# A gated DeltaNet layer on one core: token norms behind the first projection, query norms between the inversion stages, substitution rows begun behind a pair's own fifth projection

## The chip, the cores and the metric

The kernel runs on one core of one Trainium2 chip. The metric is the time of one execution of the whole program on the device, in microseconds (us); lower is better. The core has five engines that work side by side and are held together by semaphores: PE (TensorE, matrix products, with PEld for its weight loads), DVE (VectorE), ACT (ScalarE), POOL (GpSimd) and SP, whose queue issues most DMA transfers here. Each engine takes its instructions strictly in the order in which they stand in its own queue: an instruction that waits holds up all that stand behind it on that engine.

## What is computed

One layer of a decoder on 2048 tokens of width 1024, in float32: a gated DeltaNet mixer and a squared-ReLU MLP, each behind an RMS norm, and a last RMS norm. Cut to what matters here:

```python
def gated_deltanet(h, w_in, conv_w, a_log, dt_bias, norm_w, w_out):
    proj = h @ w_in                                   # 1024 -> q, k, v, z (1024 each), b, a (8 each)
    qkv = silu(causal_depthwise_conv(proj[..., :3 * 1024], conv_w))   # 4 taps
    q, k = l2_normalize(q), l2_normalize(k)           # 8 heads of 128
    beta = sigmoid(b); g = -exp(a_log) * softplus(a + dt_bias)
    o = chunk_gated_delta_rule(q, k, v, beta, g)
    o = rms(o) * norm_w * silu(z)
    return o @ w_out

# inside a chunk: (lower + eye) x = rhs is solved, lower = strict(k_beta k^T * decay)
# from chunk to chunk: v_new = u - w S ; o = q_dec S + attn v_new ; S = S * g_last + k_dec^T v_new

x = x + gated_deltanet(rms_norm(x, norm_mix), ...)
x = x + square(relu(rms_norm(x, norm_mlp) @ w_up)) @ w_down
return rms_norm(x, norm_final)
```

## The kernel before

**Blocks.** The 2048 tokens are done in two blocks (`blk` 0 and 1) of 1024. A block runs the mixer, then the output projection and the MLP. The mixer (L585) goes over two half-blocks of 512 tokens (`s` = 0 and 1), and in each over four pairs of heads (`h` = 0, 2, 4, 6). So a block has eight pairs, numbered 0 to 7 here: 0 to 3 in the first half-block, 4 to 7 in the second. Chunks have 128 tokens, so a pair has eight chunks (two heads of four), and `NC` is 8.

**One pair.** Six projections come first, in the order k, q, v, two heads each. A projection is 24 PE products of 128x512 (L117 to L119: high and low halves of the split operands, three for each of eight slices of the width) into a `pj` bank in PSUM. Its result goes through the causal convolution: ACT copies it (L303) and scales it (L304), DVE adds three taps (L307), ACT takes a tanh (L310) and DVE multiplies (L311). After the third and the fourth projection the pair's key matrices are built (`key_matrices`: PE L429, DVE L431 to L439, into `mt`), and after the fourth the substitution is set up: `invert_diagonal` solves the 32x32 diagonal blocks row by row. ACT copies `mt` four times (L322, `xc`), DVE transposes (L325, `pr`), and then DVE runs 62 short instructions, a product L333 and a sum L335 for each of 31 rows, called **rows** below. The generator hands them out in 24 steps.

**The pair before.** While a pair's projections run, the pair before it is finished, piece by piece. A generator, `prepare2`, gives one piece after each projection: the inversion's stages (`invert`, L340: DVE L345, ACT L347 `tcm`, PE L365, ACT L367 `z`, PE L373 to L376, L386 and L392), then the transposes of keys and values (PE L469, ACT L472 `vt` and `kt`) and `qe` (L463 on POOL), then PE L478 with DVE L480. After the sixth projection comes `wind_up`: the earlier pair's two gate projections (PE into `pj`, ACT L536, DVE L537), its query norms (`query_norms`: ACT L450 squares q into `sq`, PE L452 sums with a column of ones, DVE L454 adds) and then its `chain`.

**The chain** is the recurrence over four chunks for both heads: PE L496 (k times state), DVE L498 (`y`), PE L505, ACT L507 (`vr`), PE L511, DVE L512 (the new state `S`), with PE L502 and L515 into the output, then ACT L521 and L530. Each step waits for the step before it on another engine. The new pair's rows are handed out between these steps (`fill`). The chain that is run while pair n+1 is current is called chain n: chains 0 to 6 of a block stand in the loop, and chain 7 behind it, with no rows.

**Token norms.** In the first half-block, each pair also prepares 128 tokens of the next half-block: the tokens `xt` are loaded, ACT squares them (L180), DVE forms 1/sqrt by L145 and the seven instructions of `rsqrt` (L130 to L139) and scales (L181, `xn`), and PE transposes (L186) into the two `po` banks, in two groups of four; ACT L189 and DVE L190 take the results.

**What sets the order.** The code is written in one sequence. A scheduler then gives each engine its queue: it goes by the place in that sequence and by its own idea of when operands are ready. So a call that is moved in the Python code moves instructions in all queues, and not only its own.

## Time and profile before

| | before |
|---|---|
| time, median of 3 runs | 2926.35 us (2920.66 to 2933.81) |
| time of the profiled execution | 2926.04 us |
| span of its instructions | 2924.3 us |
| mean granted TensorE clock | 0.978 of full speed |
| DVE busy | 1548.9 us, 53% |
| ACT busy | 1034.0 us, 35% |
| POOL busy | 731.9 us, 25% |

The busy times are those of one profiled execution, the rest of the table is from the runs. The views that follow with the next parts are of that execution. A row of a timeline gives the start in us from the span's start, the busy time, the engine, the line of the kernel, the operation, out<-in by the program's names, partitions x elements of each, and how many instructions it joins; in brackets stands how long the engine was idle ahead of it and what it waited for.

### The profile page before, as it was taken

The numbers are of one execution on the slowest core, as the hardware profiler recorded it, in microseconds if no ns is written. First come the engines' busy times: TensorE is split into PE (matmuls) and PEld (weight loads), VectorE is DVE, ScalarE is ACT, GpSimd is POOL, SyncE is SP. The second block draws the span as 40 slices with busy tenths as digits, with TensorE's granted clock in tenths as the row PEclk, the third lists the DMA queues.
The fourth block names the chain that finished last, engine by engine and source line by source line (L and its number), as shares of the span: only waits on it lengthen the run. The fifth ranks groups of instructions, "written<-read, shape, count | busy, mean of one in ns | idle before, by whom it ended". The sixth has DMA issues, their size and how long they took to land.

```text
span 2924.3 us, 40261 instructions
## 1 busy us (share of the span) xinstructions
PE 2768.4 (95%) x15352; PEld 2325.2 (80%) x15352; DVE 1548.9 (53%) x3846; ACT 1034.0 (35%) x2338; POOL 731.9 (25%) x646
## 2 busy tenths in 40 slices
PE   7688989999999999999998999999999999999998
PEld 6577777779888888888886778787888888888887
DVE  7777777763433233333487676766544333332335
ACT  3455555554221211211246655555423112112112
POOL 6334232110042332332211111111004323323321
PEclk9889999999999999999999999999999999999999
DMA  6544455456421111111253434434662111111111
GB/s 227 182 159 168 165 177 176 169 202 226 161 72 43 58 50 38 58 51 37 65 194 142 142 122 145 145 137 148 199 230 87 44 44 58 44 44 58 48 40 65
DMA packets 81842, 337.62 MB, mean 115 GB/s; under 512 B 8817, under 2 KB 17265, under 8 KB 60145
## 3 DMA queue, kind: packets, MB, share of 16 engines
q1 hardware_dynamic: 60528, 292.98, 29.9%
q10 hardware_dynamic: 21120, 42.08, 4.2%
q8 instruction: 120, 1.97, 0.3%
q14 instruction: 74, 0.60, 0.1%
HBM read 271.98 MB, written 63.05 MB: 115 GB/s over the span
## 4 chain that ended last, share of the span: by engine, by line
PE 65%; DVE 10%; ACT 7%; issue 2%; DMA 2%; ACTq 0%; POOL 0%; POOLq 0%; DVEq 0%
PE pj L117 11%; PE pj L118 11%; PE pj L119 11%; PE kq L118 8%; PE kq L119 8%; PE kq L117 8%; ACT xc L322 2%; DVE tmp L333 2%; DVE c L307 1%; DVE tt L335 1%; DMA orw<-o_d 1%; PE kq L505 1%; PE kq L511 1%; PE kq L496 1%; PE kq L429 1%
## 5 line engine op out<-in xcount | busy, mean ns | idle before, releaser
L117 PE MATMUL pj<-hh,w 128*128 128x512 f32 x2048 | 820.7, 401 | 0.7 <-ACT c L304 0.7
L118 PE MATMUL pj<-hh,w 128*128 128x512 f32 x2048 | 817.6, 399 | 0.0
L119 PE MATMUL pj<-hl,w 128*128 128x512 f32 x2048 | 812.5, 397 | 0.0
L119 PEld LDWEIGHTS pj<-hl,w 128*128 128x128 f32 x2048 | 389.6, 190 | 79.0 <-issue 0.6
L117 PEld LDWEIGHTS pj<-hh,w 128*128 128x128 f32 x2048 | 390.1, 190 | 78.2 <-ACT c L304 1.1
L118 PEld LDWEIGHTS pj<-hh,w 128*128 128x128 f32 x2048 | 391.5, 191 | 75.8 <-issue 0.4
L742 ACT ACTIVATE r<-pj 128x512 f32<-128x512 f32 x128 | 76.9, 601 | 1059.7 <-PE pj L119 1059.7
L119 PE MATMUL kq<-dl,uh 128*128 128x512 f32 x992 | 386.8, 390 | 0.0
L118 PE MATMUL kq<-dh,ul 128*128 128x512 f32 x992 | 386.7, 390 | 0.0
L117 PE MATMUL kq<-dh,uh 128*128 128x512 f32 x992 | 386.6, 390 | 0.0
L745 DVE TENSOR_TENSOR ul<-r,uh 128x512 fp32r<-128x512 f32 x128 | 128.7, 1006 | 480.4 <-ACT uh L744 480.4
L785 DVE TENSOR_TENSOR x<-kq,x 128x512 f32<-128x512 f32 x256 | 176.8, 691 | 225.8 <-PE kq L119 223.1
L307 DVE SCALAR_TENSOR_TENSOR c<-raw,cst,c 128x512 f32<-128x512 f32 x288 | 239.9, 836 | 76.9 <-ACT c L304 73.9
L90 POOL TENSOR_SCALAR w<-wr 128x1024 fp32r<-128x1024 f32 x106 | 114.9, 1084 | 602.8 <-PE pj L119 380.5
L91 POOL TENSOR_TENSOR w<-wr,w 128x1024 fp32r<-128x1024 f32 x106 | 263.8, 2489 | 7.1
L785 DVE TENSOR_TENSOR x1h<-kq,x1h 128x512 f32<-128x512 f32 x256 | 176.7, 691 | 155.7 <-PE kq L119 155.4
L90 POOL TENSOR_SCALAR dh<-wr 128x1024 fp32r<-128x1024 f32 x62 | 64.5, 1058 | 642.0 <-PE kq L118 614.3
L117 PEld LDWEIGHTS kq<-dh,uh 128*128 128x128 f32 x992 | 186.2, 188 | 40.4 <-DVE rm L145 1.4
L118 PEld LDWEIGHTS kq<-dh,ul 128*128 128x128 f32 x992 | 186.2, 188 | 39.4
L119 PEld LDWEIGHTS kq<-dl,uh 128*128 128x128 f32 x992 | 186.2, 188 | 38.8
L333 DVE TENSOR_TENSOR tmp<-tt,pr 128x2 f32<-128x2 f32 (+30 forms) x496 | 162.1, 327 | 9.9 <-POOL pr L326 0.5
L117 PE MATMUL pj<-w,hh 128*128 128x256 f32 x512 | 147.2, 287 | 8.2 <-DMA w<-wo 5.9
(305 smaller groups left out, 3840.5 us busy)
## 6 DMA issues: line engine op xcount, KB each, us to landing
w<-wi SPq DMA_DIRECT2D x96, 1024.0 KB, 4.9
wi<-w SPq DMA_DIRECT2D x32, 1024.0 KB, 4.8
wr<-in_w_up SPq DMA_DIRECT2D x64, 512.0 KB, 3.6
w<-wo SPq DMA_DIRECT2D x32, 1024.0 KB, 5.7
wr<-in_w_down SPq DMA_DIRECT2D x64, 512.0 KB, 3.6
wr<-in_w_in SPq DMA_DIRECT2D x32, 512.0 KB, 5.8
qe<-eg_d ACTq DMA_DIRECT2D x16, 512.0 KB, 3.8
o_d<-z2s ACTq DMA_DIRECT2D x32, 256.0 KB, 3.3
```

The lines of the kernel that those rows point to most:

```text
L90: pool.tensor_scalar(dst_h, src, 1.0, 0.0, op0=MULT, op1=ADD)
L91: pool.tensor_tensor(dst_l, src, dst_h.bitcast(F32), op=SUB)
L117: pe.matmul(ps, ah, bh, start=first and i == 0, stop=False)
L118: pe.matmul(ps, al, bh, start=False, stop=False)
L119: pe.matmul(ps, ah, bl, start=False, stop=last and i == n - 1)
L307: dve.scalar_tensor_tensor(dst, raw[:, k:k + HB], cw[:, 4 * f + k:4 * f + k + 1], dst, op0=MULT, op1=ADD)
L322: act.copy(xc[r], mt[r, :, 32 * b:32 * b + 32].rearrange("p t i -> p i t").unsqueeze(2) .to_broadcast([32, 32, R, NC]))
L333: dve.tensor_tensor(tmp[:, 0:n, 0:i + 1], tt[:, 0:n, 0:i + 1], pr[:, i, 0:i + 1].unsqueeze(1).to_broadcast([P, n, i + 1]), op=MULT)
L335: dve.tensor_reduce(tt[:, 0:n, i], tmp[:, 0:n, 0:i + 1], axis=mybir.AxisListType.X, op=ADD)
L742: act.activation(r, ps, AF.Relu)
L745: dve.tensor_tensor(ul[:, hs], r, uh[:, hs].bitcast(F32), op=SUB)
L785: dve.tensor_tensor(dst, ps, dst, op=ADD)
```

## The change

There are four edits. All line numbers in the text are those of the kernel before.

1. **Token norms.** The load of `xt` is issued at the head of a pair of the first half-block, ahead of its first weights, where it was issued after the first projection. The norm itself now begins after projection 1 (before: 2), and a `yield` after `xn` parts it from the transposes, which come with steps 3 and 4 (before: 2 and 4). In the second block 1/sqrt is one power on POOL (L148) in place of `rsqrt` on DVE.
2. **Query norms** move from `wind_up`, where they stood ahead of the chain, into `prepare2`, behind the second and the third stage of the inversion. The inversion's stages begin one projection later than before.
3. **Rows.** One step of the pair's own rows is handed out after its fifth projection, and six after the sixth. The single step ahead of the gate projections goes, and the chain's first `fill` has two steps in place of three.
4. **Pair 0's rows**, which had been run out at the end of pair 0, are handed out in pair 1, 12 steps after its first projection and 24 after its second.

```diff
-    def norm_transpose(i, src, xn, wcol, hh, hl, tag):
+    def norm_transpose(i, src, xn, wcol, hh, hl, tag, use_pool=False):
...
-        dve.tensor_scalar_mul(xn, src, rstd_of(ssq))
+        dve.tensor_scalar_mul(xn, src, rstd_of(ssq, use_pool))
+        yield
...
-        yield from invert(ap, u["mt"], u["tt"], ub, t64)
-        yield
+        for i, _ in enumerate(invert(ap, u["mt"], u["tt"], ub, t64)):
+            yield
+            if i in (1, 2):
+                query_norms(ap, u, q2, i - 1)
...
-            fill(3)
+            fill(2)
...
-                fill(1)
                 z = [gate(ap, hT, h, sb)]
                 for _ in stages:
                     pass
                 z.append(gate(ap, hT, h + 1, sb))
-                for j in range(HP):
-                    query_norms(ap, u, qkv[0], j)
...
-                    next(stages, None)
+                    if s == 0:
+                        xt = wp.tile([P, D], F32, name="xt", tag="xt", bufs=4)
+                        r0 = (sb + 1) * HB + h // HP * P
+                        sp.dma_start(xt, x[r0:r0 + P, :])
...
-                            next(stages, None)
+
+                            if s == 0 and h == HP and n < 3:
+                                for _ in range(12 * n):
+                                    next(rows_of, None)
+                            if not (s == 0 and h == HP and n == 1):
+                                next(stages, None)
...
                             if s == 0 and n == 1:
-                                xt = wp.tile([P, D], F32, name="xt", tag="xt", bufs=4)
-                                r0 = (sb + 1) * HB + h // HP * P
-                                sp.dma_start(xt, x[r0:r0 + P, :])
-                            if s == 0 and n == 2:
                                 xt_steps = norm_transpose(
-                                    h // HP, xt, wp.tile([P, D], F32, name="xn", tag="xt", bufs=4), nmix, *hT2, "po")
-                            if s == 0 and n in (2, 4):
+                                    h // HP, xt, wp.tile([P, D], F32, name="xn", tag="xt", bufs=4), nmix, *hT2, "po",
+                                    blk > 0)
+                            if s == 0 and n in (1, 3, 4):
                                 next(xt_steps)
+                            if n >= 5:
+                                for _ in range((1, 6)[n - 5]):
+                                    next(rows_of)
...
-                    for _ in rows_of:
-                        pass
+                    if prev is not None:
+                        for _ in rows_of:
+                            pass
```

What this does to the queues is shown at three places. The first is PE at the beginning of chain 4 of the first block, which finishes the first pair of the second half-block. Before, with `w_4443` the second gate projection and `w_4710` the next pair's first projection:

```order
L119 MATMUL pj<-hl,w_4443 128x512
L452 MATMUL kq<-ones,sq 128x1 x4
L502 MATMUL po<-S_84,qe 128x128
L502 MATMUL po<-S_86,qe 128x128
...
L117 MATMUL pj<-hh,w_4710 128x512
L452 MATMUL kq<-ones,sq 128x1 x4
L496 MATMUL kq<-S_84,c_3235 128x128
L496 MATMUL kq<-S_86,c_3235 128x128
L118 MATMUL pj<-hh,w_4710 128x512
L119 MATMUL pj<-hl,w_4710 128x512
L505 MATMUL kq<-y,ub 128x128
```

The same place of the changed kernel, whose own line numbers are three higher in the chain (L499 is L496 of before, L508 is L505):

```order
L119 MATMUL pj<-hl,w_4482 128x512
L499 MATMUL kq<-S_84,c_3223 128x128
L499 MATMUL kq<-S_86,c_3223 128x128
L505 MATMUL po<-S_84,qe 128x128
L505 MATMUL po<-S_86,qe 128x128
L508 MATMUL kq<-y,ub 128x128 x2
L117 MATMUL pj<-hh,w_4698 128x512
L118 MATMUL pj<-hh,w_4698 128x512
L514 MATMUL kq<-vr,kt 128x128 x2
```

The eight sums with the column of ones are gone from here, and so are six products of the next projection, which now stand behind the products with `y`. The eight sums stand earlier, four behind the pair's third projection and four behind its fourth.

The second place is DVE ahead of the `y` of the same chain. Before, the last rows, with the two additions L454 and the second gate product L537 between them:

```order
L333 TENSOR_TENSOR tmp<-tt,pr 128x5x18
L454 TENSOR_SCALAR n_3427<-kq 128x4
L335 TENSOR_REDUCE tt<-tmp 128x5
L333 TENSOR_TENSOR tmp<-tt,pr 128x5x19
L537 SCALAR_TENSOR_TENSOR z2s<-z2s,pj 128x512
L335 TENSOR_REDUCE tt<-tmp 128x5
L454 TENSOR_SCALAR n_3427<-kq 128x4
L333 TENSOR_TENSOR tmp<-tt,pr 128x5x20
L498 SCALAR_TENSOR_TENSOR y<-kq,neg,vt 128x128 x2
```

The changed kernel there (L334, L336, L501 and L540 are L333, L335, L498 and L537 of before), and further up, where the transpose L326 (L325) and the taps L308 (L307) of the sixth projection stand:

```order
L326 STREAM_TRANSPOSE pr<-xc 128x1024
L308 SCALAR_TENSOR_TENSOR c_4274<-raw,cst,c_4274 128x512
L483 TENSOR_TENSOR dt__3410<-kq,dt__3410 128x512
L308 SCALAR_TENSOR_TENSOR c_4274<-raw,cst,c_4274 128x512
L334 TENSOR_TENSOR tmp<-tt,pr 128x2
L308 SCALAR_TENSOR_TENSOR c_4274<-raw,cst,c_4274 128x512
...
L336 TENSOR_REDUCE tt<-tmp 128x4
L334 TENSOR_TENSOR tmp<-tt,pr 128x5x17
L336 TENSOR_REDUCE tt<-tmp 128x5
L334 TENSOR_TENSOR tmp<-tt,pr 128x5x18
L501 SCALAR_TENSOR_TENSOR y<-kq,neg,vt 128x128 x2
L540 SCALAR_TENSOR_TENSOR z2s<-z2s,pj 128x512
```

Behind the transpose, 33 row instructions stand ahead of `y` where 37 stood, and three taps and one product L480 (L483) stand there where one tap stood. Both additions and the second gate product have left.

The third place is DVE in pair 1 of the second block, at the token norm. Before, from the mean L145 to `xn`, the `rsqrt` instructions mixed with rows of pair 0:

```order
L145 TENSOR_SCALAR rm<-ssq 128x1
...
L139 SCALAR_TENSOR_TENSOR rst<-rt,rst 128x1
L333 TENSOR_TENSOR tmp<-tt,pr 128x4x13
L311 SCALAR_TENSOR_TENSOR c_12999<-raw,c_12999 128x512
L335 TENSOR_REDUCE tt<-tmp 128x4
...
L139 SCALAR_TENSOR_TENSOR rst<-rt,rst 128x1
L335 TENSOR_REDUCE tt<-tmp 128x4
L181 TENSOR_SCALAR xn<-xt,rst 128x1024
```

In the changed kernel, one tap and one row stand between the two:

```order
L334 TENSOR_TENSOR tmp<-tt,pr 128x3x10
L145 TENSOR_SCALAR rm<-ssq 128x1
L308 SCALAR_TENSOR_TENSOR c_12938<-raw,cst,c_12938 128x512
L336 TENSOR_REDUCE tt<-tmp 128x3
L181 TENSOR_SCALAR xn<-xt,rst 128x1024
L334 TENSOR_TENSOR tmp<-tt,pr 128x3x11
```

The power L148 stands on POOL between L145 and L181. On PE the first four transposes L186 of this pair stood behind 9 of the 24 products of the third projection, and now stand behind all 24.

## Prediction

> **What bounds the kernel now.** First I read the page's busy line, then the table of windows for the mixers of the two blocks (the columns after the width are the busy time and instructions of PE, PEld, DVE, ACT and POOL, then granted clock, DMA share and GB/s):
>
> ```profile
> PE 2768.4 (95%) x15352; PEld 2325.2 (80%) x15352; DVE 1548.9 (53%) x3846; ACT 1034.0 (35%) x2338; POOL 731.9 (25%) x646
> 0.00:700.00 700.00, 610.30 (x3886) 510.71 (x3887) 506.25 (x1422) 355.05 (x831) 211.24 (x237) 0.93 0.53 182
> ...
> 1500.00:2110.00 610.00, 570.15 (x3783) 477.13 (x3782) 426.99 (x1404) 345.62 (x818) 65.81 (x139) 0.98 0.44 152
> ```
>
> PE is the bound: it idles 156 us of 2924.3. Of these 90 lie in the first mixer and 40 in the second, so 130 us is all that a reordering there can win, beside some lost clock (0.93 and 0.98). The change touches nothing elsewhere. The waits of PE by what ended them:
>
> ```profile
> PE po L186 <- DVE xn L181: 27.2, 2, 16.0
> PE kq L496 <- DVE n L454: 21.6, 8, 5.5
> PE po L186 <- ACT o L530: 11.6, 4, 8.1
> PE kq L452 <- ACT sq L450: 11.6, 4, 3.2
> ...
> PE kq L365 <- ACT z L367: 6.1, 9, 1.4
> ...
> PE po L469 <- ACT bat L232: 4.3, 2, 2.1
> PE kq L505 <- DVE y L498: 3.6, 7, 0.9
> ```
>
> The change goes at the first four rows, 72.0 us. What a removed wait is worth depends on what PE meets next, and that differs between three kinds of place.
>
> **Steady pairs: chains 3, 4 and 5 of each block, six in all.** Chain 4 of the second block, on PE, from the second key matrix (L429) to the first L505:
>
> ```profile
> 1879.39 1.14 PE L392 MATMUL kq<-ub,z 64*64 64x64 f32 x16
> 1880.46 1.16 PE L429 MATMUL kq<-c 128*128 128x128 f32 x8
> ...
> 1882.25 0.47 PE L117 MATMUL pj<-hh,w 128*128 128x512 f32 x1
> ...
> 1908.36 0.40 PE L119 MATMUL pj<-hl,w 128*128 128x512 f32 x1
> 1908.59 0.95 PE L452 MATMUL kq<-ones,sq 128*128 128x1 f32 x8
> ...
> 1913.22 0.78 PE L496 MATMUL kq<-S,c 128*128 128x128 f32 x2 [1.08 <-DVE n L454]
> ...
> 1915.04 0.80 PE L505 MATMUL kq<-y,ub 128*128 128x128 f32 x2 [0.19 <-DVE y L498]
> ```
>
> L454 is named as what PE waits for, but L454 itself stands behind rows on DVE, and so does `y` at 1914.64. DVE, then ACT:
>
> ```profile
> 1902.90 1.25 DVE L325 STREAM_TRANSPOSE pr<-xc 128x1024 f32<-128x1024 f32 x1 [2.07 <-ACT xc L322]
> 1904.07 0.71 DVE L307 SCALAR_TENSOR_TENSOR c<-raw,cst,c 128x512 f32<-128x512 f32 x1
> ...
> 1913.01 0.16 DVE L454 TENSOR_SCALAR n<-kq 128x4 f32<-128x4 f32 x1
> ...
> 1913.59 0.68 DVE L537 SCALAR_TENSOR_TENSOR z2s<-z2s,pj 128x512 f32<-128x512 f32 x1
> ...
> 1914.64 0.60 DVE L498 SCALAR_TENSOR_TENSOR y<-kq,neg,vt 128x128 f32<-128x128 f32 x2
> 1887.59 2.01 ACT L322 COPY xc<-mt 32x1024 f32<-32x1024 f32 x1 [3.35 <-DVE mt L439]
> 1889.51 0.57 ACT L303 COPY raw<-pj 128x512 f32<-128x512 f32 x1
> ...
> 1897.41 0.59 ACT L303 COPY raw<-pj 128x512 f32<-128x512 f32 x1
> ...
> 1898.74 4.12 ACT L322 COPY xc<-mt 32x1024 f32<-32x1024 f32 x2
> ```
>
> The changed queue still has 33 rows ahead of `y`. They begin when L325 is done, and L325 waits for the last of four copies `xc` on ACT (end 1902.86). In the changed ACT queue all four stand behind L303 and L304 of the fifth projection, `vt` and `kt`; before, the first stood ahead of them. The fifth projection's 24 products begin at 1882.25 and end 5.5 us later (0.23 each, as from 1908.36 to 1908.59), at 1887.8, so ACT begins L303 1.7 us earlier than at 1889.51. Into the stretch come the first copy (2.0) and L394 (a copy like L303: 0.6), out of it go L303 and L304 of the sixth projection (1897.41 to 1898.74, 1.3). That is -0.4 us: L325 all but stays. Behind it on DVE come two taps more (0.71 busy, overlapped a little: 0.67 each; one stood at 1904.07) and L480 (0.6, about as a tap), 1.9 us; out go four rows (0.25 each, by the pace between the rows at 1913.01 and 1914.64), L537 (0.6) and two L454 (0.12 each), 1.8 us. The sixth projection's taps now wait for ACT's late L304, so I take `y` 0.4 us later, with -0.4 and 1.2 as ends. **Pulling L454 away does not free `y`.**
>
> What PE does in that wait has shrunk. Two groups of sums (0.95 busy, overlapped a little: 0.8 each) have left it for the stretch between L505 and the next key matrix, where PE is busy: +1.6. Six projection products (0.23 each) stand behind L505 now: +1.4. In return L392 (1879.39 to 1880.46) leaves that stretch for the slack side, -1.1, and the next pair's wait for `z` there (nine in 6.1, 0.7 each) goes, with a few slowed products behind it, -1.0. Sum: 0.4 + 1.6 + 1.4 - 1.1 - 1.0 = **1.3 us lost** per pair. PE then stands idle for one piece, from about 1909.9 to 1915.4, 5.5 us. What a long idle costs behind it, by windows of 7 us that begin near its end (the last number but two is the clock; the first follows the 3.93 of the row ahead of it, the second the 11.28 us shown below, the third the 1.08 above):
>
> ```profile
> 413.57 0.80 PE L496 MATMUL kq<-S,c 128*128 128x128 f32 x2 [3.93 <-DVE n L454]
> 413.50:420.50 7.00, 6.75 (x33) 5.65 (x33) 5.42 (x23) 1.10 (x3) 0.00 (x0) 0.66 0.65 235
> 1565.50:1572.50 7.00, 6.98 (x27) 5.83 (x28) 5.25 (x17) 2.72 (x7) 0.38 (x2) 0.78 0.08 20
> 1915.00:1922.00 7.00, 6.96 (x47) 6.60 (x48) 5.71 (x22) 1.47 (x4) 0.00 (x0) 0.88 0.00 0
> ```
>
> In the first block the clock is at 0.66 here already, so I add 0.2; in the second it falls from 0.88 towards 0.78, 0.1 x 7 = 0.7. At worst it falls to 0.66 there too: 1.5. The term is 3 x 1.5 + 3 x 2.0 = **10.5 us lost**, with ends of 3 us won (`y` early, no clock lost) and 24 us lost (4 a pair).
>
> The Trainium skill, "TensorE: Matmul & The Clock Gate", Part 1, says that PE falls to half clock after a window of about 3.4 us without work and needs about as long of sustained work to leave it. By that rule each such wait would cost up to 1.7 us, and the six 10 us in place of my 2.7, for a time 7.5 us above the one below. The 3.93 us wait with 0.66 behind it agrees; the 11.28 us wait, with 0.78 behind it, does so only in part.
>
> **Chain 6 of each block.** PE's wait there is for `sq`, behind the copies on ACT, not for rows:
>
> ```profile
> 640.03 1.84 PE L452 MATMUL kq<-ones,sq 128*128 128x1 f32 x8 [2.55 <-ACT sq L450]
> ```
>
> The sums leave, so 2.55 us (the other block alike) goes and `y` moves up by at most that; the products behind L505 take about 1.1 back. 1.5 each, **3 us won**, ends 0 and 6.
>
> **First half-blocks.** The first long wait of each block is for `xn`. In the second block, PE first, then DVE, PE again:
>
> ```profile
> 1565.52 1.12 PE L186 MATMUL po<-cst,xn 128*128 128x128 f32 x4 [11.28 <-DVE xn L181]
> 1561.30 0.15 DVE L145 TENSOR_SCALAR rm<-ssq 128x1 f32<-128x1 f32 x1
> 1564.72 0.74 DVE L181 TENSOR_SCALAR xn<-xt,rst 128x1024 f32<-128x1024 f32 x1
> 1589.18 0.45 DVE L345 STREAM_TRANSPOSE tr<-tt 128x256 f32<-128x256 f32 x1
> 1590.36 0.69 PE L365 MATMUL kq<-tcm,mt 32*32 32x32 f32 x16 [0.30 <-ACT tcm L347]
> 1599.58 1.16 PE L429 MATMUL kq<-c 128*128 128x128 f32 x8
> 1619.59 0.67 PE L505 MATMUL kq<-y,ub 128*128 128x128 f32 x4
> L148 POOL TENSOR_TENSOR rst<-rm,mhalf 128x1 f32<-128x1 f32 x20 | 12.3, 617 | 121.5 <-DVE rm L145 116.6 <-DVE dnwh L63 4.9
> 77.00:104.00 27.00, 11.04 (x41) 8.76 (x40) 24.96 (x62) 10.37 (x22) 12.69 (x13) 0.69 0.58 212
> ```
>
> `xn` is late because DVE is full of rows and taps, not because the norm begins late. From L145 to L181 are 3.4 us; with a power of 0.6 on POOL, one tap and one row I take 1.2, so `xn` comes 2.2 earlier, and PE has done 15 more products (3.4 us) by then. L345 ends the rows at 1589.18; without `rsqrt`, and with fewer gaps, I take it 2.7 us earlier. In the changed queue the second key matrix stands about 5 us behind the first L365 and not 10 (1590.36 to the end of the row at 1599.58), so the copies `xc`, which hold up L325, end about 7 us earlier. `y` has 13 rows (2.6 us) and L537 (0.6) ahead of it where it had L454 and L537. I put L505 at 1612.8, 6.8 us earlier, with six products (1.4) still to do: 5.4 us won. The later two pairs lose a short wait of L186 for `o` (the row's 11.6 less the 8.1) and half of L469's for the gates (2.1): I take 3.5 together. **9 us won**, ends 0 and 20.
>
> In the first block `rsqrt` stays, and DVE is full around the wait (24.96 of 27 us, the last row). `xn` keeps its time, 15 products are done by then (3.4), the wait for `sq` in chain 0 (3.2, the longest of its row) goes, and 13 rows come ahead of `y` (2.6): 4. In pair 2 the 8.1 us wait of L186 for `o` becomes one of L365 for `tcm`, which stands now where L186 stood, 1 won; in pair 3 about 3 with L469's wait of 2.1 and the lost clock behind it. **8 us won**, ends 0 and 20.
>
> The earlier load costs nothing that I see: it lands several us ahead of any use, and a projection lasts 5.5 us, longer than the few us by which weights are moved back in SP's queue. If that cover is gone, it is 1 us for each of eight pairs, which lies inside the ends.
>
> **Sum.** 10.5 - 3 - 9 - 8 = -9.5 us on 2926.04, the profiled execution, which is 0.3 us under the median: **2917 us**.
>
> **Rivals.** (a) *The waits go and nothing takes their place.* The four rows are 72.0 us; the mixers' clock says some 10 us more. For it: four edits at four causes. Against it: `y` behind 33 rows, DVE at 92% around the first wait. Even half of it gives 2926 - 36 = 2890; a third, 2902. (b) *The steady pairs decide.* `y` keeps its time behind the rows, PE's filling work is gone, and the clock falls at each chain. At 4 us a pair it is 24 lost, and if DVE's backlog eats what the first half-blocks win down to 4, the time is 2926 + 24 - 4 - 3 = 2943. It decides from 3.3 us a pair on, where it outweighs the 20 won. For it: `y` follows L325 by 11.7 us of rows and taps without a gap of note, so DVE has nothing to give. (c) *It doesn't do what it says*: the scheduler's queues give back what the code moves, and gains and losses cancel within 3 us: 2926. The changed PE queue, with the long wait only moved, speaks for it.
>
> **Chances.** Forecast (2917, own range 2905 to 2930) 0.45, (a) 0.25, (b) 0.17, (c) 0.13. 0.5%, 14.6 us, is about what a measurement of this kernel can tell from no change. Under 2911.7 lie (a) and a third of the forecast, less a little: 0.38. Above 2941 lie most of (b): 0.15. Between: 0.47. The range that leaves 2 in 10 out is 2888 to 2943.
>
> **What would show it.** Right: PE's row L496 <- L454 gone, and L505 <- `y` grown from 3.6 to over 25 us, with some 5 us at each of chains 3 to 5; L325 in place; L186 <- `xn` nearer 18 than 27 us. Wrong: `y` 3 us or more ahead of its old place, or L186's wait under 5 us (then (a)); a pair's period, L505 to L505, over 3 us above its old one (then (b)); a new row of waits for weights, in which case my word on SP falls.

## The result, and the profile after

The changed kernel takes 3015.41 us (median of 4 runs, 3008.12 to 3024.25) against 2923.51 us for the kernel before (4 runs, 2916.66 to 2933.81). The ratio is **1.031**, with a 95% interval of 1.0285 to 1.0336: 3.1% slower, above the whole range of the prediction. Of the times below, one execution of the kernel with `z` on DVE, 3304.93 us at a granted clock of 0.786 where its others had 0.958 to 0.962, is left out.

The page of the changed kernel, its busy line, and then its waits of PE (engine, tile and line that wait, what ended the wait; us in total, times, longest):

```profile
PE 2827.4 (94%) x15352; PEld 2379.6 (79%) x15352; DVE 1569.7 (52%) x3814; ACT 1030.7 (34%) x2338; POOL 736.6 (24%) x650
PE kq L508 <- DVE y L501: 68.1, 14, 10.1
PE kq L366 <- ACT z L368: 30.4, 9, 6.8
PE kq L366 <- ACT tcm L348: 18.3, 5, 8.1
PE pj L118 <- POOL w L91: 11.6, 4, 6.0
PE po L187 <- DVE xn L181: 3.5, 2, 2.8
```

(Behind the edits lines are shifted: L508 is L505 of before, L501 is `y` (L498), L366 is L365, L368 is `z` (L367), L430 is L429, L453 is L452, L518 is L515, L326 is L325.) The waits for `n` and most of that for `xn` are gone, as intended. In their place stand `y` (3.6 before), `z` (6.1 before), `tcm`, and a new row for weights. But waits are the smaller part: of the 98.2 us by which the span grew (2924.3 to 3022.5), PE's idle time has 39.2 (155.9 to 195.1) and its **busy time 59.0**, for the same 15352 products. The same work ran at a slower clock: 0.954 granted on average, where the kernel before had 0.978.

One page is one execution, and this is the longest of the four (3024.25). The other three were 8 to 16 us shorter, at clocks of 0.956 to 0.959. So a difference in busy time between two pages is good to some 10 us, no better.

Where? The projections are the same in both kernels, so the start of a given projection bounds the same work, but for 13 to 17 small products of the inversion that cross a boundary. Four windows for each kernel: first and second half-block of the first block, then of the second, each second one from the second projection of the fifth pair to the second gate projection behind the last. Before, then after:

```profile
19.26:352.88 333.62, 280.22 (x1654) 229.22 (x1652) 259.35 (x713) 160.79 (x366) 138.56 (x133) 0.90 0.50 174
352.88:657.74 304.86, 280.48 (x1812) 235.83 (x1809) 216.51 (x630) 164.82 (x382) 62.74 (x82) 0.96 0.53 182
1483.38:1786.72 303.34, 278.27 (x1720) 228.43 (x1718) 226.03 (x757) 168.86 (x392) 37.42 (x81) 0.97 0.41 148
1786.72:2074.55 287.83, 274.31 (x1811) 230.57 (x1809) 199.21 (x630) 164.76 (x381) 31.17 (x64) 0.98 0.43 151
```

```profile
18.26:364.57 346.31, 288.95 (x1637) 236.00 (x1637) 263.09 (x708) 158.12 (x365) 138.27 (x132) 0.88 0.48 170
364.57:700.74 336.17, 293.51 (x1825) 248.84 (x1824) 224.20 (x636) 164.75 (x381) 63.65 (x83) 0.89 0.49 165
1527.14:1844.38 317.24, 293.51 (x1703) 242.62 (x1702) 224.59 (x720) 168.06 (x394) 42.69 (x84) 0.92 0.40 142
1844.38:2175.20 330.82, 297.85 (x1826) 252.79 (x1824) 209.40 (x638) 165.19 (x380) 31.23 (x65) 0.89 0.38 132
```

The widths differ by +12.7, +31.3, +13.9 and +43.0, 100.9 in all. In the first half-blocks (+26.6) PE's idle time is about what it was (78.5 and 81.1 us in the two together): its waits moved and its products got slower. In the second half-blocks (+74.3), the steady ones, half is idle time and half the clock, which fell from 0.96 and 0.98 to 0.89.

Now one steady pair of the second block, the one the prediction followed from L505 at 1915.04. The changed kernel's PE, from the inversion of the next pair, behind that chain's first L508 (at 1986.45), to the first L508 of the next chain:

```profile
2008.21 0.69 PE L366 MATMUL kq<-tcm,mt 32*32 32x32 f32 x16
...
2015.41 1.06 PE L366 MATMUL kq<-tcm,mt 32*32 32x32 f32 x16 [3.12 <-ACT z L368]
...
2020.84 1.70 PE L453 MATMUL kq<-ones,sq 128*128 128x1 f32 x8
...
2036.57 1.16 PE L430 MATMUL kq<-c 128*128 128x128 f32 x8
...
2071.15 1.22 PE L508 MATMUL kq<-y,ub 128*128 128x128 f32 x4 [4.88 <-DVE y L501]
```

Windows of the same stretch (after the width the busy times; the last number but two is the clock), from the wait for `z` on:

```profile
2015.40:2020.80 5.40, 5.38 (x26) 4.39 (x27) 1.93 (x3) 3.13 (x9) 0.00 (x0) 0.50 0.00 0
2020.80:2026.90 6.10, 6.10 (x67) 5.48 (x65) 2.76 (x9) 2.82 (x6) 0.76 (x2) 0.50 0.50 175
2026.90:2034.60 7.70, 7.70 (x24) 6.17 (x24) 3.33 (x14) 0.99 (x2) 0.21 (x1) 0.67 0.00 0
```

The same places before, from the inversion's first products to the first key matrix, and PE's rows of the second key matrix and the next L505:

```profile
1930.40:1937.05 6.65, 5.91 (x39) 4.63 (x38) 2.98 (x14) 5.83 (x18) 0.95 (x3) 1.00 0.50 172
1937.05:1944.70 7.65, 7.51 (x99) 5.98 (x99) 5.25 (x8) 4.78 (x10) 2.49 (x5) 1.00 0.47 192
```

```profile
1952.38 0.49 PE L429 MATMUL kq<-c 128*128 128x128 f32 x2
1987.24 0.49 PE L505 MATMUL kq<-y,ub 128*128 128x128 f32 x2 [0.87 <-DVE y L498]
```

From the second key matrix to the next L505 is 34.86 us before (1952.38 to 1987.24) and 34.58 after (2036.57 to 2071.15): nothing lost, although PE now stands still for 4.88 us of it in one piece. From L505 to that key matrix is 37.34 before (1915.04 to 1952.38) and 50.12 after (1986.45 to 2036.57): **12.8 us lost in one pair, all on the other side of L505.** Behind the 3.12 us wait for `z` PE ran at half clock for 11.5 us and at 0.67 for 7.7 more; against full clock that is 0.5 x 11.5 + 0.33 x 7.7 = 8.3 us. With the wait itself, 3.1, that makes 11.4 of the 12.8.

### The profile page after: what moved, and what is told of

It reads as the page before. It is cut to its first block, busy times and chain, and to the rows that moved or that the text cites. A ratio compares the mean times of both kernels' runs of the same rounds, so it can differ in the third digit from the quotient of the medians.

```text
span 3022.5 us, 40216 instructions
## 1 busy us (share of the span) xinstructions
PE 2827.4 (94%) x15352; PEld 2379.6 (79%) x15352; DVE 1569.7 (52%) x3814; ACT 1030.7 (34%) x2338; POOL 736.6 (24%) x650
## 4 chain that ended last, share of the span: by engine, by line
PE 69%; DVE 17%; ACT 9%; DMA 3%; issue 2%; POOL 0%; ACTq 0%; SPq 0%; DVEq 0%; POOLq 0%
PE pj L117 12%; PE pj L119 12%; PE pj L118 12%; PE kq L119 8%; PE kq L118 8%; PE kq L117 7%; DVE tmp L334 4%; ACT xc L323 3%; DVE c L308 3%; DVE tt L336 3%; DMA orw<-o_d 1%; PE kq L430 1%; PE kq L453 1%; PE kq L508 1%; PE kq L514 1%
## 5 line engine op out<-in xcount | busy, mean ns | idle before, releaser
L118 PE MATMUL pj<-hh,w 128*128 128x512 f32 x2048 | 826.7, 404 | 11.6 <-POOL w L91 11.6
L117 PE MATMUL pj<-hh,w 128*128 128x512 f32 x2048 | 834.6, 408 | 0.3 <-DVE hl L174 0.3
L119 PE MATMUL pj<-hl,w 128*128 128x512 f32 x2048 | 825.4, 403 | 0.0
L118 PEld LDWEIGHTS pj<-hh,w 128*128 128x128 f32 x2048 | 397.3, 194 | 91.9 <-POOL w L91 13.1
L119 PEld LDWEIGHTS pj<-hl,w 128*128 128x128 f32 x2048 | 397.0, 194 | 81.3
L117 PEld LDWEIGHTS pj<-hh,w 128*128 128x128 f32 x2048 | 397.8, 194 | 79.8 <-issue 0.6
L308 DVE SCALAR_TENSOR_TENSOR c<-raw,cst,c 128x512 f32<-128x512 f32 x288 | 242.7, 843 | 57.7 <-ACT c L305 54.0
L91 POOL TENSOR_TENSOR w<-wr,w 128x1024 fp32r<-128x1024 f32 x106 | 263.6, 2487 | 7.5
L90 POOL TENSOR_SCALAR w<-wr 128x1024 fp32r<-128x1024 f32 x106 | 114.2, 1077 | 606.3 <-PE pj L119 372.1
L90 POOL TENSOR_SCALAR dh<-wr 128x1024 fp32r<-128x1024 f32 x62 | 63.9, 1047 | 639.3 <-PE kq L118 611.5
L117 PEld LDWEIGHTS kq<-dh,uh 128*128 128x128 f32 x992 | 186.2, 188 | 40.3 <-DVE rm L145 1.2
L334 DVE TENSOR_TENSOR tmp<-tt,pr 128x2 f32<-128x2 f32 (+30 forms) x496 | 185.3, 374 | 10.1
```

The costliest lines, as they stand in the source:

```text
L90: pool.tensor_scalar(dst_h, src, 1.0, 0.0, op0=MULT, op1=ADD)
L91: pool.tensor_tensor(dst_l, src, dst_h.bitcast(F32), op=SUB)
L117: pe.matmul(ps, ah, bh, start=first and i == 0, stop=False)
L118: pe.matmul(ps, al, bh, start=False, stop=False)
L119: pe.matmul(ps, ah, bl, start=False, stop=last and i == n - 1)
L308: dve.scalar_tensor_tensor(dst, raw[:, k:k + HB], cw[:, 4 * f + k:4 * f + k + 1], dst, op0=MULT, op1=ADD)
```

## The experiments

Two theories were open. *Cover*: the query sums, ahead of the chain, were filling work while `y` was on its way; without them PE idles. *Clock*: the sums' new place, among the inversion's small products, makes the wait for `z` long enough to drop the clock, and what follows is too thin to lift it. The kernels were timed against runs of the kernel before on the same chip, whose median lay between 2925 and 2931 us.

**Undoing one part at a time.** The query sums put back ahead of the chain:

```diff
-        for i, _ in enumerate(invert(ap, u["mt"], u["tt"], ub, t64)):
-            yield
-            if i in (1, 2):
-                query_norms(ap, u, q2, i - 1)
+        yield from invert(ap, u["mt"], u["tt"], ub, t64)
...
+                for j in range(HP):
+                    query_norms(ap, u, qkv[0], j)
                 os_ = chain(ap, h, u, fill)
```

> The changed kernel with the query norms alone put back ahead of the chain (stages, rows and token norms as changed). Theory C (clock): PE's products run slower because waits now stand right ahead of stretches of small products, so that the clock stays low; 59 of the 98 us are busy time of PE. The wait for y (68 us) gets its filler back and shrinks to about 30, the wait for z (30 us) stays, with the low clock behind it: 2985 us. Theory W (waits): the loss is the idle time itself, and most of it is y: 3015 - 40 = 2975 us, with PE's busy time unchanged at 2827. If the query norms have no part in it: 3015.

Measured 2947.47, ratio 1.0063 (1.0041 to 1.0085). Its waits (`n` is written at L455 there) and its busy line:

```profile
PE kq L496 <- DVE n L455: 32.6, 9, 7.5
PE kq L366 <- ACT z L368: 20.3, 10, 4.0
...
PE 2787.1 (95%) x15352; PEld 2338.4 (79%) x15352; DVE 1562.1 (53%) x3814; ACT 1032.8 (35%) x2338; POOL 740.0 (25%) x650
```

68 us come back; of the 80.4 by which the profiled span is shorter, 40.3 are PE's busy time. The wait for `y` falls to 5.9, and the old one for `n` returns with 32.6. That is more than either theory gave (40 by the waits, 30 by the clock): both parts came back. It is not the wait for `z` alone, which is still 20.3 us. By half-blocks, in the windows above, this kernel is 2.1 and 1.8 us shorter than the kernel before in the first ones (331.54 and 301.56 us), and 12.9 and 10.4 longer in the second (317.78 and 298.20). The stages begun one projection earlier again:

```diff
                 query_norms(ap, u, q2, i - 1)
+        yield
...
                     stages = stages_of(*prev) if prev is not None else iter(())
+                    if not (s == 0 and h == HP):
+                        next(stages, None)
```

> The changed kernel with the inversion's stages begun one projection earlier again, as before (query norms stay between the stages). Theory C: the wait for z falls from 30 to under 10 us and that for tcm from 18 to under 8, and the clock behind them recovers as well: PE busy falls by 30 us or more, time 2950. Theory W: the same waits go and nothing else: 3015 - 32 = 2983, PE busy unchanged. If the stages have no part: 3015.

Measured 2987.6, ratio 1.0209 (1.0192 to 1.0226), 28 us less. Its waits in the inversion:

```profile
PE kq L366 <- ACT tcm L348: 36.7, 12, 8.2
...
PE kq L366 <- ACT z L368: 0.3, 1, 0.3
```

The wait for `z` is gone, as both theories said, but the one for `tcm` has doubled where it was to shrink, and PE's busy time falls by 16.7 us, to 2810.7, where theory C had 30 or more. So it takes the later start of the stages to make PE wait for `z`: 0.3 us with the sums moved and the stages as before, 20.3 with the stages moved and the sums as before, 30.4 with both. The rows handed out as before:

```diff
-            fill(2)
+            fill(3)
...
+                fill(1)
                 z = [gate(ap, hT, h, sb)]
...
-                            if n >= 5:
-                                for _ in range((1, 6)[n - 5]):
-                                    next(rows_of)
```

> The changed kernel with the rows handed out as before (one step ahead of the gate projections, three in the chain's first fill, none behind projections five and six). Theories C and W: rows stood ahead of y before as well (37 against 33), so y's wait stays near 68 us and the time within 10 us of 3015. Theory R (rows begun early hold up y): y's wait falls by 40 us, time 2970.

Measured 2977.62, ratio 1.0176 (1.0161 to 1.0191): 38 us less. Theory R gave about that, but by the wait for `y`, which hardly moves (66.6 us); PE's busy time falls by 36.1 to 2791.3, and the wait for `tcm` from 18.3 to 6.0. The token norms as before (load, split and power of 0.6 taken back):

```diff
         dve.tensor_scalar_mul(xn, src, rstd_of(ssq, use_pool))
-        yield
...
-                            if s == 0 and n in (1, 3, 4):
+                            if s == 0 and n in (2, 4):
```

> The changed kernel with the token norms as before (load behind the first projection, norm from step 2, both groups of transposes at steps 2 and 4, 1/sqrt on DVE in both blocks). Theory S (SP's queue goes in twos): PE's waits for split weights (11.6 us) go, with about 8 us of slow products behind them, and the waits for xn come back (up to 24 us): between 3005 and 3030. If the token norms were the main loss: under 2980.

Measured 3010.94, ratio 1.0278 (1.0257 to 1.0299): 4 us less, no more than the intervals leave open. The waits for weights go, and 22.5 us for `xn` come back. Last, query sums, rows and stages all as before, so that only the token norms and the first pair's rows are changed:

> The changed kernel with query norms, rows and stages all as before; what is left of the change is the token norms and pair 0's rows in pair 1. Undone one at a time, the three gave 68, 38 and 28 us. If they are independent: 3015 - 134 = 2881 us. If they pay for the same waits: 2925 to 2940. By the waits for xn (27.2 us before) the token norms alone should give 10 to 17 us against before: 2912.

Measured 2944.67, ratio 1.0044 (1.0024 to 1.0064). That is the time with the query sums alone put back: with those ahead of the chain, moving rows and stages together costs nothing that these intervals show. Their 38 and 28 us exist only beside the moved sums.

**One part alone, on the kernel before.** First the token norms; then the same without the earlier load (`xt` issued behind the first projection, as before):

```diff
-        dve.tensor_scalar_mul(xn, src, rstd_of(ssq))
+        dve.tensor_scalar_mul(xn, src, rstd_of(ssq, use_pool))
+        yield
...
+                    if s == 0:
+                        xt = wp.tile([P, D], F32, name="xt", tag="xt", bufs=4)
...
-                            if s == 0 and n in (2, 4):
+                            if s == 0 and n in (1, 3, 4):
```

> The kernel before with the token norms' edit alone (early load, parting yield, steps 1, 3 and 4, power on POOL in the second block); pair 0's rows are run out at the end of pair 0 as before. If handing pair 0's rows out in pair 1 is what costs u_qrs its 14 us: 2925 to 2932, and PE's wait for tcm (20.3 us in u_qrs) falls under 10. If the early load is: 2945, with PE's waits for split weights near 13 us as in u_qrs.

> As a_only, with the load of xt back behind the first projection, so that only the norm's place and the power are changed. Theory S (the early load sets the weights in twos): PE's waits for split weights go (8.4 and 5.0 in u_qrs), about 10 us with the slow products behind them; against a_only 8 to 15 us less, 2918 to 2935. By the prediction's own sum for the first half-blocks: 2909.

Measured 2938.39 (1.0042, 1.0026 to 1.0058) and 2930.61 (1.0008, 0.9993 to 1.0022). The norms win nothing by themselves: without the earlier load the wait for `xn` falls from 27.2 to 14.7 us, and that for `vt`, which PE meets next, grows from 13.3 to 19.1. The earlier load costs 7.8 us. That rests on the ten executions of each kernel; the two profiled ones, 2931.19 and 2932.64, don't show it. With the load PE waits 5.3 us for weights (`w`, L91), once for 5.0; without it, as in the kernel before, it never does. In the changed kernel there are four such waits. The longest, by SP's queue, POOL and PE:

```profile
67.66 4.82 SPq L104 DMA_DIRECT2D wi<-w  x2
72.58 0.37 SPq L626 DMA_DIRECT2D xt<-in_x  x1
73.05 1.97 SPq L100 DMA_DIRECT2D wr<-in_w_in  x2
79.75 1.05 POOL L90 TENSOR_SCALAR w<-wr 128x1024 fp32r<-128x1024 f32 x1 [2.78 <-DMA wr<-in_w_in]
...
85.02 2.34 POOL L91 TENSOR_TENSOR w<-wr,w 128x1024 fp32r<-128x1024 f32 x1
87.41 0.79 PE L118 MATMUL pj<-hh,w 128*128 128x512 f32 x1 [6.04 <-POOL w L91]
```

`wr` is the load of weights that POOL then splits into `w` (L90, L91), and `wi` stores the split ones. From the first early `xt`, at 3.16 us, both stand in SP's queue in twos (`wi`, `wi`, then `wr`, `wr`), where the kernel before has one `wi` and one `wr` in turn. So a load stands behind two stores, each of which waits for its split: here the loads are issued at 73.05, POOL waits for them until 79.75, its L91 then stands behind `qe`, and PE has no weights for 6.04 us. The kernel before had issued a load at 71.80 and the next at 79.60, and has no such wait.

Then the query sums alone:

```diff
-        yield from invert(ap, u["mt"], u["tt"], ub, t64)
+        for i, _ in enumerate(invert(ap, u["mt"], u["tt"], ub, t64)):
+            yield
+            if i in (1, 2):
+                query_norms(ap, u, q2, i - 1)
...
-                for j in range(HP):
-                    query_norms(ap, u, qkv[0], j)
```

> The kernel before with one part of the change alone: the query sums between the inversion stages; token norms, rows and stages stay as they were. Theory A, the placing costs by itself: undoing it gave 68 us in the changed kernel, so some 60 us here, 2975 to 3000, with the wait of PE for y above 40 us. Theory K, it costs only together with the rows and stages that were moved: with those back at their places 2925 to 2945, and a wait for y below 20 us.

Measured 2967.04, ratio 1.0146 (1.0124 to 1.0168), between the two theories' numbers: the placing costs 41 us by itself. Two of its waits and its busy line:

```profile
PE kq L508 <- DVE y L501: 53.2, 9, 10.3
...
PE kq L365 <- ACT z L367: 0.2, 1, 0.2
...
PE 2783.0 (94%) x15352; PEld 2343.4 (79%) x15352; DVE 1569.2 (53%) x3846; ACT 1029.5 (35%) x2338; POOL 731.4 (25%) x646
```

Of the 41.0 us by which its span is longer, 26.4 are idle time and 14.6 busy time: more cover than clock. The wait for `y` is 50 us longer than before, less the 21.6 for `n` and the 11.6 for `sq` that are gone; `tcm` has 15 more (19.6) and `vr` 12.1. The wait for `z` has gone, from 6.1 to 0.2. So of the change's 92 us, 41 come with the sums alone and 13 with norms and first pair (the ratio 1.0044 above); the other 38 arise only when sums, stages and rows are moved together. The intervals of the three ratios leave some 10 us open in that 38.

**The place of the sums.** Three kernels move them within the changed one: one sum put back ahead of the chain, both one stage earlier, both one stage later.

```diff
-            if i in (1, 2):
-                query_norms(ap, u, q2, i - 1)
+            if i in (0, 1):
+                query_norms(ap, u, q2, i)
```

(that is the second of the three; the first has `if i == 1` with head 0 here and head 1's sum ahead of `chain`, the third `i in (2, 3)` with `i - 2`).

> The changed kernel with the second head's query sum put back ahead of the chain, the first left behind the z stage. If both cost alike: halfway between 3015 and 2947, 2981. If what counts is that one sum ahead of the chain covers the wait for y: near 2950. If one sum in the inversion already slows it as both do: 3000 to 3015.

> The changed kernel with both query sums one stage earlier, behind the first and the second stage of the inversion. If their place in the inversion costs by delaying z on ACT and PE: dearer than the change, 3025 to 3040, and the wait for z above 30 us. If it costs by their absence ahead of the chain: as the change, 3005 to 3020.

> The changed kernel with both query sums one stage later, behind the third and the fourth stage of the inversion. If their place in the inversion costs by delaying z: 2965 to 2990, and the wait for z falls below 15 us. If it costs by their absence ahead of the chain: as the change, 3005 to 3020, with the wait for y still above 60 us.

Measured 2991.6 (1.0215, 1.0194 to 1.0237), **2978.14** (1.0178, 1.016 to 1.0195) and 2999.64 (1.0248, 1.0222 to 1.0274). The third lies between its two theories: the wait for `z` falls to 22.1 only, and that for `y` stays at 66.4. The middle one fell against what I expected of both theories: sums placed earlier were to be dearer or the same, and are 37 us cheaper. Its waits and its busy line:

```profile
PE kq L508 <- DVE y L501: 71.6, 12, 10.6
PE kq L366 <- ACT z L368: 20.2, 8, 6.8
...
PE 2795.6 (94%) x15352; PEld 2354.6 (79%) x15352; DVE 1569.2 (53%) x3814; ACT 1031.4 (35%) x2338; POOL 743.1 (25%) x650
```

It does the same work, and waits for `y` even longer than the change does (71.6 to 68.1). What differs most is PE's busy time, 31.8 us less, then the wait for `z`, 10 us shorter, and that for `tcm`, 7 us shorter. In the second half-blocks its clock is 0.94 where the change has 0.89. The same steady pair as above shows how, PE's rows and then the clock:

```profile
1977.35 0.95 PE L453 MATMUL kq<-ones,sq 128*128 128x1 f32 x8
1978.23 0.69 PE L366 MATMUL kq<-tcm,mt 32*32 32x32 f32 x16
...
1984.35 0.69 PE L366 MATMUL kq<-tcm,mt 32*32 32x32 f32 x16 [2.03 <-ACT z L368]
```

```profile
1984.30:1987.30 3.00, 2.95 (x26) 2.52 (x27) 1.96 (x3) 2.93 (x8) 0.00 (x0) 1.00 0.00 0
1987.30:1996.10 8.80, 8.80 (x90) 7.30 (x88) 6.17 (x23) 4.68 (x11) 1.55 (x3) 1.00 0.35 121
```

One group of sums now stands ahead of the first L366, and ACT works on through its queue meanwhile: the second L366 begins 5.4 us behind the end of the first, where it was 6.5, the wait is 2.03 us instead of 3.12, and the clock stays at 1.00. From the end of that wait to the second key matrix are 13.0 us (to 1997.34) where the change has 21.2, with one group of sums (0.9) less in it. **That is the clock theory with the cover ahead of the chain held fixed.** All executions agree: the span times what the clock lacks of 1, which is the time that a low clock can have cost at most, is 123 to 139 us in the four of the changed kernel, 101 to 107 in the five of this one, 76 to 103 in the eight with the sums put back, and 61 to 88 in those of the kernel before. So some 37 of the 68 us that the query sums cost are mostly clock, with shorter waits for `z` and `tcm`. Of what is left to the kernel with the sums ahead of the chain, 31 us by the medians (2978 to 2947) and 34 by the two pages, 26 are idle time and 8 busy time: mostly cover. One sum put back gives 24, about a third of the two together and not half, with 6.8 us of waits for `z` and 24.5 for `tcm`; whether the other one alone would give the rest was not tried.

**Why PE waits for `z`.** ACT in the changed kernel, between the two groups of L366, and then PE at the same place before:

```profile
2008.72 2.17 ACT L533 ACTIVATE o<-po,rq 128x128 f32<-128x128 f32 x8 [2.04 <-DVE rq L139]
...
2015.00 0.36 ACT L368 COPY z<-kq 32x256 f32<-32x256 f32 x1
```

`z`'s operands are there at 2008.9, and its copy of 0.36 us stands behind 6 us of other work on ACT.

```profile
1930.45 0.69 PE L365 MATMUL kq<-tcm,mt 32*32 32x32 f32 x16
...
1937.07 0.59 PE L365 MATMUL kq<-tcm,mt 32*32 32x32 f32 x13 [0.72 <-ACT z L367]
```

But `z` was hardly quicker before: the second group began 5.9 us behind the end of the first (1931.14 to 1937.07), against 6.5 now. What changed more is what PE has to do meanwhile: 22 products of a projection (5.0 us) stood between the two groups, and 14 (3.2 us) stand there now. Of the 2.4 us by which this wait grew, 0.6 are `z` and 1.8 are missing filling work, here too. In the steady pairs of the second block 22 products and a group of sums stand there with the sums alone moved, 20 products with the sums put back, and 14 with stages and sums both moved. The copies of `z` on DVE instead, run twice:

```diff
-            act.copy(z[rd], v(ps, rd, 32))
+            dve.tensor_copy(z[rd], v(ps, rd, 32))
```

> The changed kernel with the two small copies z (L367) on DVE, idle there, in place of ACT, whose queue holds them up; the scheduler then moves the second L365 earlier. Theory C: the wait for z goes (30 to under 8 us), and the inversion's small products behind it run at full clock: PE busy falls by 25 us or more, time 2960. Theory W: the wait alone goes, 3015 - 24 = 2991, PE busy stays at 2827.

> The same kernel as z_dve, for a profile that can be compared. It came out at 2997, 19 us under the changed kernel. Theory C: PE's wait for z is not gone in all places, and PE's busy time has fallen by more than the wait. Theory W: the wait for z has fallen by 15 to 25 us and PE's busy time stands at 2820 or more.

Measured 2995.11 (1.0217, 1.0172 to 1.0262) and 2999.22 (1.0244, 1.0211 to 1.0277). The wait falls from 30.4 to 17.3 us and the time by 16 to 20, but PE's busy time only by 7.5, to 2819.9, less than two pages can tell: a shorter wait alone does not bring the clock back, as theory W had it.

**Useless products as filling work.** Two kernels add 128x512 products whose results nobody reads: 20 ahead of the first `y` of each chain, and 14 between the two groups of L366.

```diff
+            if t == 0:
+                warm(20)
             fill(2)
```

```diff
             act.copy(z[rd], v(ps, rd, 32))
+            if a == 0:
+                warm(14)
```

> The changed kernel with 20 useless products of 128x512 (4.6 us at full clock) on PE between the first L496 and the rest of each chain, in the wait for y; nothing else moves. The result does not use them. Theory C: the clock stays up through the wait, so that the chain behind it runs at full speed: 11.25 us from the first L505 to the last of chain 5 in the second block become about 9.0, the time falls by 20 to 30 us (2990) although PE has 73 us more to do. Theory W (only idle time counts): the wait is filled with useless work, time the same, or 5 to 15 us longer where the wait was shorter than 4.6 us: 3015 to 3030.

> The changed kernel with 14 useless products of 128x512 (3.2 us) between the two groups of L365; the scheduler puts the 14 real products that stood there behind the second group, so that 24 products in place of 10 stand between the wait for z and the small products. The wait itself stays. Theory C: the 24 products bring the clock back before the small products begin; the window from L374 to the second L430 shows a clock near 1.0 in place of 0.65, and the useless 45 us (14 x 0.228 x 14) are paid back by more than half: 3020 to 3035. Theory W: 3015 + 45 = 3060.

Measured 3040.82 (1.0377, 1.034 to 1.0415) and 3054.89 (1.0438, 1.0408 to 1.0468). Neither is a clean test as timed, since the added products cost more than they save, and the first moved rows on DVE too (the wait for `y` fell to 19.3, and one of 42.1 for the state `S` came up). The second can be read from its profile, the stretch behind a 3.23 us wait for `z`, and its busy line:

```profile
2037.70:2047.70 10.00, 9.97 (x48) 8.23 (x48) 2.64 (x4) 4.08 (x12) 0.19 (x1) 0.68 0.01 2
2047.70:2050.30 2.60, 2.60 (x59) 2.27 (x59) 1.66 (x5) 1.89 (x4) 0.19 (x1) 1.00 0.86 262
...
PE 2847.0 (93%) x15576; PEld 2397.3 (79%) x15576; DVE 1572.9 (52%) x3814; ACT 1032.5 (34%) x2338; POOL 730.2 (24%) x650
```

With large products behind the wait the clock is back within these 10 us, and the small ones behind them run at 1.00, where the change has 0.50. The 224 added products would be 51.5 us at 0.23 each; the trace has 67.0 for them (459 ns on average against 393 at the median), as some ran slowly. Without them PE is busy 2780.0 to 2795.5 us, 32 to 47 less than in the change, at about the same idle time (200.7 us against 195.1): that is the clock. The earlier sums gave 32. Both figures carry the spread between executions, so they agree in kind, not to the microsecond.

**The query sums behind the inversion**, at the end of the last piece, behind L480:

```diff
+        for j in range(HP):
+            query_norms(ap, u, q2, j)
         u.update(ub=ub, qe=qe, kt=kt, vt=vt, at=dt_, k2=k2, gt=gt, c0=c0)
```

> The changed kernel with the query norms at the end of prepare2 (behind L478 and L480, ahead of the gate projections) in place of between the stages. They are then neither among the small products of the inversion nor in the wait for y. Theory C (low clock where waits meet small products): the stretch behind the wait for z loses 1.6 us of sums and two waits on ACT, PE busy falls by some 20 us, time 2990. Theory F (what counts is that the sums and six products no longer fill the wait for y): no gain, 3010.

Measured 2973.13, ratio 1.0158 (1.0111 to 1.0206). The wait for `y` falls to 15.4, and one for `sq` comes up with 39.1: there the sums wait for the squares on ACT. PE's busy time falls by 26.4, to 2801.0, and the time by 42: more than theory C gave, and not theory F. No kernel tried beats the one before.

## Why the prediction was wrong

**What held.** The row for `n` went, and the wait for `y` grew from 3.6 to 68.1 us, with 4.9 to 5.2 at each steady chain of the second block and 7.5 to 10.1 at those of the first, where 3.9 had been lost to `n`; L325 stayed, 21.9 us behind the key matrix where it was 22.4; from the key matrix to L505 a pair takes as long as before, 34.58 to 34.86, where 0.4 us more was forecast. "Pulling L454 away does not free `y`" is what the profile shows.

**The step that failed is the other half of the steady pairs' term**, from L505 to the next key matrix. It had 1.6 for the sums and 1.4 for six products, less 1.1 for L392 and less 1.0 because "the next pair's wait for `z` there (nine in 6.1, 0.7 each) goes": 0.9 us. Measured are 12.8 us in the pair followed above. The wait for `z` did not go but grew, from 6.1 to 30.4 us over the kernel, with 3.12 in this pair. It does go with the sums alone moved (0.2 us); what the forecast left out is that the stages begin a projection later, which beside the moved sums takes eight filling products from between the two groups of L365. And the clock, for which 0.2 or 0.7 us a pair were added behind the wait for `y` alone, fell a second time behind the wait for `z`, where small products follow: 8.3 us. 1.6 + 1.4 - 1.1 + 3.1 + 8.3 is 13.3, near the 12.8. The six pairs and chain 6 were put at 10.5 lost and 3 won, 7.5 us; the second half-blocks, in which they lie, lost 74.3. Rival (b), the steady pairs losing, came nearest, and its sign came: this pair's period, L505 to L505, grew from 72.20 to 84.70 us. Its mechanism, "PE's filling work is gone, and the clock falls at each chain", is part of what the runs showed; the rest is the wait and the clock in the inversion, and its 4 us a pair was a third of what came.

**First half-blocks.** 9 and 8 us won were forecast; 13.9 and 12.7 were lost. The wait for `xn` did fall, from 27.2 to 3.5, below the 5 us that I had set as a sign for rival (a). But `tcm` took its place (18.3, the longest 8.1), as the forecast had it for one pair only, and PE's idle time there is about the same (78.5 and 81.1), while its busy time rose by 24 us. The moved sums cost here too: with them back ahead of the chain, the first half-blocks are 14.8 and 15.7 us shorter than in the changed kernel, and 2.1 and 1.8 shorter than before. So what the forecast put at 8 and 9 is worth about 2 each without the sums, because PE meets other waits where `xn` was (`tcm`, and `hl` at L472, 9.8 us where it was 1.3), and the sums take that and more: half clock follows 6.83 us for `z` at 292.6 and 8.11 for `tcm` at 201.2.

**The load.** "The earlier load costs nothing that I see" was wrong: the row of waits for weights that I had named as the sign against it came, with 11.6 us over four waits, and alone on the kernel before it costs 7.8. It is a term that I had bounded at 1 us for each of eight pairs, so the size lay at that bound; the reason given for nothing, that a projection (5.5 us) is longer than the shift, did not hold once weights went out in twos and POOL's splits came late.

**The rule on the clock.** The Trainium skill, "TensorE: Matmul & The Clock Gate", Part 1, puts the fall to half clock behind about 3.4 us without work. The waits for `y` near 5 us agree in kind: behind the 4.88 us wait the clock was 0.62 for 6.9 us. But half clock also followed waits of 3.12 and 2.29 us here, under that window, so that the sum by the page, 10 us for six waits for `y`, left out those for `z`.

**What stays open.** Rows and stages cost 38 and 28 us beside the moved sums and nothing without them. For the rows the busy time says clock (36.1 of them); for the stages it says so of 16.7 in 28. Why the three interact was not separated. They make the 38 us left over above.

## What to carry to other kernels

Before a step that issues work on the bounding engine is moved, look at both ends: at the old place it may be what fills a wait that isn't its own, and at the new one it may lengthen a wait in a stretch of small products, where a lost clock may not be won back soon (here 0.50 for 11.5 us). Price the clock at each wait that the change makes or lengthens, not only at the longest, and compare the busy time of the same instructions before looking at waits: here 59 of 98 us were no wait at all. A load issued earlier displaces what stands behind it in its queue, and the order there shows whether the stream that feeds the bounding engine still comes one by one.

## What the hardware showed that I had not expected

The clock did not fall at one length of wait. Two waits for `z` in the same execution of the changed kernel, each with the clock of the window behind it (last number but two), in which PE stood still nowhere:

```profile
625.94 1.05 PE L366 MATMUL kq<-tcm,mt 32*32 32x32 f32 x16 [2.29 <-ACT z L368]
626.00:635.00 9.00, 9.00 (x71) 7.89 (x72) 3.28 (x6) 5.10 (x14) 2.19 (x4) 0.50 0.01 2
1777.17 0.69 PE L366 MATMUL kq<-tcm,mt 32*32 32x32 f32 x16 [2.91 <-ACT z L368]
1777.20:1782.20 5.00, 5.00 (x75) 4.64 (x75) 3.44 (x7) 4.86 (x13) 0.81 (x2) 1.00 0.33 103
```

Behind 2.29 us it was at half, behind 2.91 us full. Nor did it return after one length of time: behind a wait of 3.20 us at 1857.20 it was 0.59 for 4.1 us and then 1.00, and behind the 3.12 us wait of the pair above 0.50 for 11.5 us and 0.67 for 7.7, although the same kinds of products followed. What sets the two points was not tried.
